# Output chunks gathered before the first and between the first and second of seven products, and transpositions taken singly, in the gated blocks of a two-layer decoder

## The chip, the cores and the metric

The kernel runs on one core of one Trainium2 chip. The metric is the device time of one execution in microseconds; the figure given is the median of several runs. TensorE runs at one of two clock levels, 2.4 or 1.2 GHz.

## What is computed

The reference is a decoder of two layers with 256 tokens and width 1024, in float32. Each layer has a gated block (SwiGLU), an attention (stick-breaking in the first layer, sparse attention with three branches in the second), and another gated block. The change touches the four gated blocks alone:

```python
def _swiglu(x, w_in, w_out):
    a, b = jnp.split(x @ w_in, 2, axis=-1)
    return (jax.nn.silu(a) * b) @ w_out

h = h + 0.5 * _swiglu(_rmsnorm(h, ffn1_norm[layer]), ffn1_w_in[layer], ffn1_w_out[layer])
```

The inner width is 2816. The program names the gated blocks f10 and f20 (before and after the attention of layer 0), f11 and f21 (of layer 1).

## The kernel before

**Weights.** A unit is 128 rows by 1024 columns of float32, 512 KB. The class `Weights` loads units in one fixed order over SP's queue into five raw buffers (`wraw`, line 104). `pump` (line 146) makes two tiles of a unit: the upper part `wh` (ScalarE, line 166) and the lower part `wl`, the rest after rounding (VectorE, line 168). There are six buffers for each, so at most six units are converted ahead of TensorE, and a conversion waits until TensorE has used the unit six places before. The activations are split the same way, and a product is three matmuls for each piece of the sum: upper by upper, upper by lower, lower by upper (`mm3`, lines 222 to 224).

**Blocks.** The inner width has 11 blocks of 256. A plain block j takes four units and gives, for each half of the tokens, 256 gate and 256 value columns. `gate` (line 481) makes g = silu(.) * (.) of it: ScalarE's part at lines 487 and 490 (`sil`), VectorE's at lines 488 and 491. `gtrans` (line 494) transposes the block's g with four small matmuls into a bank `gTp` and evacuates it into an upper part (`gTh`, ScalarE, line 503) and a lower part (`gTl`, VectorE, line 504). These are the stationary operand of the second matrix.

**Pairs.** Two blocks j and j+1 are computed together by seven products in place of eight (`pair`, line 552). The activations are cut into four quarters (two halves of the tokens by two halves of the width), the weights into b11, b21 (block j) and b12, b22 (block j+1), two units each. A product is 12 matmuls of 128x512 on two units. p1 uses b11; p5 and p6 use kept sums of b11, b12, b22; p3 uses b22; p7 uses b12 + b22; p2 uses b21; p4 the last kept sum. The sums are made in two ways: a tile `keep` is loaded, converted, and then a DMA that GpSimd issues adds the next weight to it (line 133), and later VectorE adds to it (line 173). A conversion of `keep` therefore waits for such an addition. ScalarE's queue is in order, so everything behind that conversion waits too.

p1 and p2 go to a bank c11, p6 and p7 to cu (which first takes a copy of c11), p5 and p3 to c12, p4 to c21. Copies stand between: after p5 ScalarE copies c12 (line 582) before p3 adds to that bank; after p6 it copies cu before p7 adds to it; after p7 it copies cu to c21 (line 608) for p4. Four gates follow: of block j+1 after p6 and after p7, of block j after p2 and after p4.

**Output chunks.** A chunk (line 702) is one unit of the second matrix: 12 matmuls into the four banks of `o`. Chunk k reads the transposed g of block k // 2. TensorE has eight banks: four of the pool `acc`, which hold a pair's results until the output begins and the output from then on, two of pool `z`, two of `aux`. While the output is open, c11 and cu live in `z`, c12 and then c21 in one bank of `aux`, and all transpositions share the other.

**The order.** The table `FAST` (line 27) sets for each gated block the sequence. A number is a plain block; (j, n, m) and (j, n) with positive n is a pair that has the plain blocks n and m among its products; (j, -n) is a pair with n output chunks among its products. The same table gives the order of units (`fast`, line 229) and of the computation (`fast_blocks`, line 621). There are seven pairs with output chunks: two each in f10, f20 and f21 with seven chunks, one in f11 with six. In f10 the first of them follows the pair of blocks 3 and 4, in f20 and f21 that of blocks 2 and 3, in f11 plain block 7. `late` holds blocks whose g is not yet transposed; `trans` (line 638) transposes all of them. After a pair without chunks it holds two. `beside` runs side work of the attention that follows f11. The order written here is the program's; a scheduler with its own cost model then sets each engine's queue and may exchange neighbours.

Of the kernel before, what the change touches and what calls it, by code (L numbers as in the profile page):

```python
# [190 lines left out]
def build(tc, ctx, a, out):  # L191
# [37 lines left out]
    def fast(l):  # L229

        b = lambda j, k: [a[l[:2] + "i" + l[2]][4 * j + 2 * k + i] for i in range(2)]
        v, r, pairs = [], range(2), 0
        outs = [a[l[:2] + "o" + l[2]][i] for i in range(2 * NB)]
        for j in FAST[l]:
            if not isinstance(j, tuple):
                v += b(j, 0) + b(j, 1)
                continue
            j, *n = j
            b11, b21, b12, b22 = b(j, 0), b(j, 1), b(j + 1, 0), b(j + 1, 1)
            key = lambda i: (j, pairs % 2, i)  # L240
            kept = lambda last=False: [Sum(key(i), last=last) for i in r]
            u22 = [Unit(b22[i], key=key(i)) for i in r]
            tail_ = [Unit(b12[i], plus=b22[i]) for i in r] + [Unit(b21[i], key=key(i)) for i in r] + kept(True)
            v += [Sum(key(i), load=b11[i], then=b12[i]) for i in r]
            if n[0] < 0:
                c = lambda n: [outs.pop(0) for _ in range(n)]
                v += c(2) + kept() + c(1) + u22 + kept() + c(1) + tail_[0:2] + c(1) + tail_[2:4] + c(1) + tail_[4:6] + c(-n[0] - 6)
            elif len(n) == 2:
                v += b(n[0], 0) + b(n[0], 1) + kept() + b(n[1], 0) + u22 + kept() + b(n[1], 1) + tail_
            else:  # L250
                v += b(n[0], 0) + kept() + u22 + b(n[0], 1) + kept() + tail_
            pairs += 1
        if l == "f11":
            return v + outs
        v += outs
        units.extend(v)
# [206 lines left out]
    def ffn(l, hT, rs, post, targets, side=(), pool=None, start=None, room=new_room):  # L463
# [3 lines left out]
        with ExitStack() as es:  # L467
# [153 lines left out]
            def fast_blocks():  # L621
# [13 lines left out]

                    return first, second

                def trans():
                    while late:
                        gtrans(late.pop(0))  # L640

                def beside():
                    if side:
                        side.pop(0)()

                for j in FAST[l][2 if start else j0:]:
# [9 lines left out]
                    p1, p5, p3, p6, p7, p2, p4 = pair(j, q, n < 0)  # L656
                    if m:
                        p1(), trans()
                        f, g = block(n, [zbank("n") for _ in range(2)])
                        f(), g(), p5(), gtrans(n)  # L660
                        n, = m
                        f, g = block(n, [zbank("n") for _ in range(2)])
                        f(), p3(), p6(), g(), p7(), p2(), gtrans(n), p4()
                        late.append(j + 1)
                    else:
                        p1(), beside(), chunk(), trans(), chunk(), beside(), p5(), chunk(), beside(), p3(), p6(), beside()
                        chunk(), beside(), p7(), chunk(), p2(), chunk(), gtrans(j + 1), p4()
                        for _ in range(-n - 6):
                            chunk()
                    late.append(j)  # L670
                taken["one"] = False
                trans_last.extend(late)

            trans_last, late = [], [0, 1] if start else [j0 - 1]
# [27 lines left out]
            def chunk():  # L702
                ws.append(W.take())
                for t in range(2):
                    for hf in range(2):
                        mm(len(ws) - 1, t, hf)
                W.done()
                W.pump()

            fast_blocks()  # L710
            n = 2 * NB - 4
# [869 lines left out]
```

## Time and profile before

| | |
|---|---|
| median of 3 runs | 1040.67 us (1040.11 to 1043.32) |
| profiled execution | 1042.57 us, its span 1040.5 us |
| TensorE, matmuls | 1005.7 us busy, 97% of the span, 5033 instructions |
| TensorE, weight loads | 839.7 us (beside matmuls) |
| VectorE | 785.9 us |
| ScalarE | 660.0 us |
| GpSimd | 123.9 us |
| mean granted clock | 0.989 of 2.4 GHz |
| HBM read | 197.99 MB, 191 GB/s over the span |

A matmul of 128x512 takes about 0.39 us from its start to its modelled end, but the next one starts 0.227 us after it, since matmuls are pipelined. Starts, not durations, give the length of a stretch. The profile names engines PE (TensorE), PEld (its weight loads), DVE (VectorE), ACT (ScalarE), POOL (GpSimd) and SP (the queue that issues most DMAs), and leaves buffer numbers out of tile names. Idle time of TensorE stands in brackets behind a row, with what ended it.

### The profile page before, as it was taken

What the parts mean: (1) busy time and instruction counts of PE and PEld (TensorE: products, weight loads), DVE (VectorE), ACT (ScalarE), POOL (GpSimd) and SP (SyncE); (2) the same over time, 40 slices, a digit from 0 to 9 for tenths busy, and PEclk for the clock granted to TensorE, in tenths of its full rate; (3) what the DMA queues carried; (4) which work ended last, traced back from release to release, by engine and by line L of the source; (5) the groups of instructions that cost most, each with busy time, mean ns of one, the idle gap of its engine ahead of it and who ended that gap; (6) DMA issues with size and microseconds to landing.
All of it is one profiled execution on the core that took longest, in us unless ns stands there. A gap on an engine that the chain in (4) does not pass through costs nothing.

```text
span 1040.5 us, 14104 instructions
## 1 busy us (share of the span) xinstructions
PE 1005.7 (97%) x5033; PEld 839.7 (81%) x5033; DVE 785.9 (76%) x1077; ACT 660.0 (63%) x1043; POOL 123.9 (12%) x180
## 2 busy tenths in 40 slices
PE   9997999999999997999999999999989999979998
PEld 6785888898978876888888888788878888858887
DVE  7877778778869778885777678864798768768873
ACT  6755666677857656664555676653689746657651
POOL 0101000000001000100117111100056500010000
PEclk9998999999999999999999999999989999989999
DMA  8978778454336787787565667865441156887861
GB/s 324 316 214 226 208 214 263 135 192 140 123 122 208 211 247 205 187 256 224 184 200 158 203 203 226 239 213 158 146 145 38 41 178 187 228 221 203 236 225 40
DMA packets 57093, 199.95 MB, mean 192 GB/s; under 512 B 6464, under 2 KB 7488, under 8 KB 57024
## 3 DMA queue, kind: packets, MB, share of 16 engines
q1 hardware_dynamic: 50976, 177.93, 51.1%
q0 software_dynamic: 5760, 20.97, 12.0%
q8 instruction: 39, 0.64, 0.3%
q14 instruction: 30, 0.25, 0.1%
q10 hardware_dynamic: 288, 0.16, 0.1%
HBM read 197.99 MB, written 1.05 MB: 191 GB/s over the span
## 4 chain that ended last, share of the span: by engine, by line
PE 68%; DMA 9%; issue 7%; DVE 7%; ACT 5%; POOL 3%; SPq 0%; POOLq 0%; ACTq 0%; DVEq 0%
PE o L222 8%; PE o L224 8%; PE o L223 8%; DVE wl L168 3%; PE c L222 3%; PE c L223 3%; PE c L224 3%; DMA wraw<-in_f1i 3%; DMA keep<-in_f1i 3%; ACT wh L166 2%; DMA wraw<-in_f2i 2%; PE a L224 2%; PE a L222 2%; PE a L223 2%; DMA keep<-in_f2i 2%
## 5 line engine op out<-in xcount | busy, mean ns | idle before, releaser
L168 DVE TENSOR_TENSOR wl<-wraw,wh 128x1024 fp32r<-128x1024 f32 (+2 forms) x310 | 374.0, 1218 | 111.2 <-ACT wh L166 108.0
L166 ACT ACTIVATE wh<-wraw 128x1024 fp32r<-128x1024 f32 (+2 forms) x312 | 322.2, 1045 | 150.7 <-PE o L224 54.2
L166 ACT ACTIVATE wh<-keep 128x1024 fp32r<-128x1024 f32 x80 | 84.3, 1057 | 62.3 <-DMA keep<-in_f2i 24.6
L168 DVE TENSOR_TENSOR wl<-keep,wh 128x1024 fp32r<-128x1024 f32 x80 | 97.4, 1222 | 27.1 <-ACT wh L166 25.8
L222 PE MATMUL o<-wh,gTh0f 128*128 128x512 f32 x192 | 76.6, 399 | 5.4 <-DVE g L491 5.4
L222 PE MATMUL a<-wh,hT_f 128*128 128x512 f32 x192 | 76.1, 396 | 0.0
L223 PE MATMUL o<-wl,gTh0f 128*128 128x512 f32 x192 | 75.3, 392 | 0.0
L224 PE MATMUL o<-wh,gTl0f 128*128 128x512 f32 x192 | 75.1, 391 | 0.0
L224 PE MATMUL a<-wh,hT_f 128*128 128x512 f32 x192 | 75.0, 390 | 0.0
L223 PE MATMUL a<-wl,hT_f 128*128 128x512 f32 x192 | 75.0, 390 | 0.0
L222 PE MATMUL o<-wh,gTh1f 128*128 128x512 f32 (+1 forms) x160 | 62.7, 392 | 0.0
L224 PE MATMUL o<-wh,gTl1f 128*128 128x512 f32 (+1 forms) x160 | 62.0, 388 | 0.0
L223 PE MATMUL o<-wl,gTh1f 128*128 128x512 f32 (+1 forms) x160 | 61.9, 387 | 0.0
L173 DVE TENSOR_TENSOR keep<-keep,wraw 128x1024 f32<-128x1024 f32 x40 | 48.7, 1221 | 15.2 <-DMA wraw<-in_f2i 11.2
L342 POOL TENSOR_TENSOR rstd<-rss,mhalf 128x1 f32<-128x1 f32 x12 | 8.4, 704 | 364.8 <-DVE rss L340 364.8
L222 PEld LDWEIGHTS o<-wh,gTh0f 128*128 128x128 f32 x192 | 36.3, 189 | 13.8 <-DVE g L491 6.7
L222 PE MATMUL n<-wh,hT_f 128*128 128x512 f32 x112 | 44.3, 395 | 0.0
L224 PE MATMUL n<-wh,hT_f 128*128 128x512 f32 x112 | 43.7, 390 | 0.0
L223 PE MATMUL n<-wl,hT_f 128*128 128x512 f32 x112 | 43.6, 390 | 0.0
L498 PE MATMUL gTp<-cst,g 128*128 128x128 f32 x176 | 28.0, 284 | 15.6 <-DVE gTl0f L504 15.0
L224 PEld LDWEIGHTS o<-wh,gTl0f 128*128 128x128 f32 x192 | 36.3, 189 | 7.7
L224 PEld LDWEIGHTS a<-wh,hT_f 128*128 128x128 f32 x192 | 36.1, 188 | 7.6
(352 smaller groups left out, 2467.8 us busy)
## 6 DMA issues: line engine op xcount, KB each, us to landing
wraw<-in_f1i SPq DMA_DIRECT2D x76, 512.0 KB, 4.5
wraw<-in_f2i SPq DMA_DIRECT2D x76, 512.0 KB, 4.4
wraw<-in_f1o SPq DMA_DIRECT2D x44, 512.0 KB, 4.4
wraw<-in_f2o SPq DMA_DIRECT2D x44, 512.0 KB, 4.5
wraw<-in_sbqk SPq DMA_DIRECT2D x16, 512.0 KB, 3.4
keep<-in_f2i SPq DMA_DIRECT2D x12, 512.0 KB, 5.0
keep<-in_f2i POOLq DMA_DIRECT2D x12, 512.0 KB, 7.4
wraw<-in_f2i POOLq DMA_DIRECT2D x12, 512.0 KB, 5.9
```

Of the source, the lines that this page charges most:

```text
L166: nc.scalar.activation(hi[:, 0:n], raw[:, 0:n], AF.Copy)
L168: e.tensor_tensor(lo[:, 0:n], raw[:, 0:n], hi[:, 0:n].bitcast(F32), op=OP.subtract)
L173: nc.vector.tensor_tensor(t, t, raw, op=OP.add)
L222: nc.tensor.matmul(o, xh, wh, start=start, stop=False, skip_group_check=True)
L223: nc.tensor.matmul(o, xh, wl, start=False, stop=False, skip_group_check=True)
L224: nc.tensor.matmul(o, xl, wh, start=False, stop=stop, skip_group_check=True)
L342: nc.gpsimd.tensor_tensor(r[:, 0:1], s, mhalf[:, 0:1], op=OP.pow)
L498: nc.tensor.transpose(p[:, c * 256 + t * P:c * 256 + (t + 1) * P], gs[j, t][:, c * P:(c + 1) * P], ident)
```

## The change

The chunks of a pair move. Before, one stood behind each of p1, p5, p6, p7, p2, with a second one before p5 and the last ones at the end. Now n - 5 chunks (two, in f11 one) come ahead of p1, four between p1 and p5, one between p6 and p7, and none elsewhere. The order of the units follows. `trans` takes a number: between p1 and p5 one transposition is made after the first of the four chunks and one after the third, where before two were made together after the first chunk. Block j of a pair without chunks is put at the front of `late`. f11's side work has six places in a pair in place of five.

```diff
@@ -241,10 +241,10 @@
             kept = lambda last=False: [Sum(key(i), last=last) for i in r]
             u22 = [Unit(b22[i], key=key(i)) for i in r]
             tail_ = [Unit(b12[i], plus=b22[i]) for i in r] + [Unit(b21[i], key=key(i)) for i in r] + kept(True)
-            v += [Sum(key(i), load=b11[i], then=b12[i]) for i in r]
+            c = lambda n: [outs.pop(0) for _ in range(n)]
+            v += c(max(-n[0] - 5, 0)) + [Sum(key(i), load=b11[i], then=b12[i]) for i in r]
             if n[0] < 0:
-                c = lambda n: [outs.pop(0) for _ in range(n)]
-                v += c(2) + kept() + c(1) + u22 + kept() + c(1) + tail_[0:2] + c(1) + tail_[2:4] + c(1) + tail_[4:6] + c(-n[0] - 6)
+                v += c(4) + kept() + u22 + kept() + c(1) + tail_
             elif len(n) == 2:
                 v += b(n[0], 0) + b(n[0], 1) + kept() + b(n[1], 0) + u22 + kept() + b(n[1], 1) + tail_
             else:
@@ -635,8 +635,8 @@
 
                     return first, second
 
-                def trans():
-                    while late:
+                def trans(n=2):
+                    for _ in range(min(n, len(late))):
                         gtrans(late.pop(0))
 
                 def beside():
@@ -662,12 +662,15 @@
                         f, g = block(n, [zbank("n") for _ in range(2)])
                         f(), p3(), p6(), g(), p7(), p2(), gtrans(n), p4()
                         late.append(j + 1)
+                        late.insert(0, j)
                     else:
-                        p1(), beside(), chunk(), trans(), chunk(), beside(), p5(), chunk(), beside(), p3(), p6(), beside()
-                        chunk(), beside(), p7(), chunk(), p2(), chunk(), gtrans(j + 1), p4()
-                        for _ in range(-n - 6):
+                        for _ in range(-n - 5):
                             chunk()
-                    late.append(j)
+                        p1(), beside()
+                        for _ in range(2):
+                            chunk(), trans(1), chunk(), beside()
+                        p5(), p3(), beside(), p6(), beside(), chunk(), beside(), p7(), p2(), gtrans(j + 1), p4()
+                        late.append(j)
                 taken["one"] = False
                 trans_last.extend(late)
```

**TensorE, start of f10's first pair with chunks.** c21 is p4 of the pair before, c11 is p1, o00 the first quarter of a chunk (the number behind wh is the unit), gTp a transposition, c12 is p5. Before:

```order
L222 MATMUL c21_779<-wh33_786,hT_0_120 128x512
...
L222 MATMUL c11_878<-wh34_798,hT_0_120 128x512
...
L222 MATMUL o00_874<-wh36_829,gTh0f10_442 128x512
...
L498 MATMUL gTp_920<-cst_78,g_731 128x128
...
L222 MATMUL o00_874<-wh37_852,gTh0f10_442 128x512
...
L498 MATMUL gTp_927<-cst_78,g_834 128x128
...
L222 MATMUL c12_953<-wh38_864,sums_385 128x512
```

Now:

```order
L222 MATMUL c21_779<-wh33_786,hT_0_120 128x512
...
L222 MATMUL o00_878<-wh34_798,gTh0f10_442 128x512
...
L222 MATMUL o00_878<-wh35_817,gTh0f10_442 128x512
...
L222 MATMUL c11_914<-wh36_829,hT_0_120 128x512
...
L222 MATMUL o00_878<-wh38_868,gTh0f10_442 128x512
...
L498 MATMUL gTp_957<-cst_78,g_837 128x128
...
L222 MATMUL o00_878<-wh39_894,gTh0f10_442 128x512
...
L222 MATMUL o00_878<-wh40_910,gTh0f10_442 128x512
...
L498 MATMUL gTp_1000<-cst_78,g_731 128x128
...
L222 MATMUL o00_878<-wh41_922,gTh0f10_442 128x512
...
L222 MATMUL c12_1026<-wh42_934,sums_385 128x512
```

Two chunks stand ahead of p1, and two chunks stand between the transpositions in place of one.

**ScalarE, the same place.** `wh<-keep` is a conversion of a kept unit, sil_870 and sil_874 the gate after p4, cu the copy after p1. Before:

```order
L166 ACTIVATE wh37_852<-wraw37_803 128x1024
L503 ACTIVATE gTh1f10_842<-gTp_837 128x512
L166 ACTIVATE wh38_864<-keep_761 128x1024
L490 ACTIVATE sil_870<-c21_779,rstd_348 128x256
L166 ACTIVATE wh39_886<-keep_773 128x1024
L166 ACTIVATE wh40_898<-wraw40_856 128x1024
L575 ACTIVATE cu_879<-c11_878 128x512
L166 ACTIVATE wh41_915<-wraw41_868 128x1024
L166 ACTIVATE wh42_946<-wraw42_890 128x1024
L503 ACTIVATE gTh0f10_442<-gTp_920 128x512
```

Now:

```order
L166 ACTIVATE wh37_855<-keep_802 128x1024
L503 ACTIVATE gTh1f10_845<-gTp_840 128x512
L166 ACTIVATE wh38_868<-wraw38_821 128x1024
L490 ACTIVATE sil_874<-c21_779,rstd_348 128x256
L166 ACTIVATE wh39_894<-wraw39_834 128x1024
L166 ACTIVATE wh40_910<-wraw40_860 128x1024
L166 ACTIVATE wh41_922<-wraw41_872 128x1024
L166 ACTIVATE wh42_934<-keep_790 128x1024
L575 ACTIVATE cu_915<-c11_914 128x512
L166 ACTIVATE wh43_953<-keep_802 128x1024
L166 ACTIVATE wh44_976<-wraw44_926 128x1024
L503 ACTIVATE gTh0f10_442<-gTp_957 128x512
```

The first conversion that waits for an accumulating DMA (wh38 before, wh42 now) has moved from ahead of the gate to four conversions behind it.

**TensorE and ScalarE, p5 to p4 of that pair, now.** On TensorE c12 is p5 and p3, cu is p6 and p7, c11 is p2, c21 is p4; g_1105 and g_1155 are the gates of block j+1 after p6 and after p7:

```order
L222 MATMUL c12_1026<-wh42_934,sums_385 128x512
...
L222 MATMUL cu_915<-wh46_1019,sums_385 128x512
...
L222 MATMUL c12_1026<-wh44_976,sums_385 128x512
...
L222 MATMUL cu_915<-wh47_1033,sums_385 128x512
...
L498 MATMUL gTp_1187<-cst_78,g_1105 128x128
L222 MATMUL c21_1126<-wh53_1120,hT_0_120 128x512
...
L222 MATMUL c21_1126<-wh54_1133,hT_0_120 128x512
L498 MATMUL gTp_1187<-cst_78,g_1155 128x128
```

On ScalarE, from the copy after p7 to the gate's part:

```order
L608 ACTIVATE c21_1126<-cu_915 128x512
L166 ACTIVATE wh56_1164<-wraw56_1124 128x1024
L166 ACTIVATE wh57_1176<-keep_1137 128x1024
L487 ACTIVATE sil_1154<-x_1152,rstd_348 128x256
L490 ACTIVATE sil_1183<-c11_914,rstd_336 128x256
```

The chunk between p5 and p3 is gone, and the scheduler has put the first four matmuls of p6 there; behind p7 two chunks are gone, and one of the four transpositions and seven matmuls of p4 stand ahead of the other three.

## Rows read from the trace of the kernel before

**Rows 1.** The page, parts 1 and 2: busy time of the engines (share of the span, instructions), and TensorE's granted clock in 40 slices of the span, in tenths.

```profile
PE 1005.7 (97%) x5033; PEld 839.7 (81%) x5033; DVE 785.9 (76%) x1077; ACT 660.0 (63%) x1043; POOL 123.9 (12%) x180
PEclk9998999999999999999999999999989999989999
```

**Rows 2.** The list of waits, TensorE's alone: the waiting line and what it waited for, us in total, times, longest.

```profile
PE gTp L498 <- DVE gTl0f L504: 15.0, 3, 5.8
PE o L222 <- DVE g L491: 5.4, 3, 2.6
```

**Rows 3.** The instructions in order of time, TensorE: start and duration in us, line, tiles, and in brackets the idle time before it and what ended it. f10, f10, f20, f20, f21, f21.

```profile
92.09 0.80 PE L222 MATMUL o<-wh,gTh0f 128*128 128x512 f32 x1 [2.63 <-DVE g L491]
101.42 0.66 PE L498 MATMUL gTp<-cst,g 128*128 128x128 f32 x4 [3.76 <-DVE gTl0f L504]
389.57 0.50 PE L222 MATMUL o<-wh,gTh0f 128*128 128x512 f32 x1 [1.66 <-DVE g L491]
399.24 1.11 PE L498 MATMUL gTp<-cst,g 128*128 128x128 f32 x4 [5.48 <-DVE gTl0f L504]
921.72 0.50 PE L222 MATMUL o<-wh,gTh0f 128*128 128x512 f32 x1 [1.12 <-DVE g L491]
931.62 1.12 PE L498 MATMUL gTp<-cst,g 128*128 128x128 f32 x4 [5.75 <-DVE gTl0f L504]
```

**Rows 4.** The table by stretches: from and to in us, length, busy us of each engine (instructions), granted clock (1.00 is 2.4 GHz), DMA share, GB/s.

```profile
91.70:95.10 3.40, 3.01 (x9) 2.52 (x10) 1.71 (x3) 1.33 (x2) 0.00 (x0) 0.50 0.74 264
102.00:105.40 3.40, 3.40 (x10) 2.63 (x10) 2.24 (x3) 1.26 (x2) 0.89 (x1) 0.51 0.85 282
398.90:402.30 3.40, 3.06 (x10) 2.58 (x11) 3.15 (x4) 0.60 (x1) 0.87 (x1) 0.50 0.95 337
928.00:934.80 6.80, 3.18 (x10) 2.70 (x11) 6.43 (x7) 2.52 (x4) 0.86 (x1) 0.50 0.90 254
```

**Rows 5.** In order of time, ScalarE at the start of the first pair with chunks in f10.

```profile
90.16 1.06 ACT L166 ACTIVATE wh<-keep 128x1024 fp32r<-128x1024 f32 x1 [4.67 <-DMA keep<-in_f1i]
93.77 1.06 ACT L166 ACTIVATE wh<-keep 128x1024 fp32r<-128x1024 f32 x1 [2.19 <-DMA keep<-in_f1i]
98.09 0.57 ACT L503 ACTIVATE gTh0f<-gTp 128x512 fp32r<-128x512 f32 x1
```

**Rows 6.** In order of time, TensorE: the first transposition of such a pair, in f10 and in f21.

```profile
93.54 1.06 PE L498 MATMUL gTp<-cst,g 128*128 128x128 f32 x4
922.52 0.60 PE L498 MATMUL gTp<-cst,g 128*128 128x128 f32 x4
```

**Rows 7.** In order of time, f10, f20 and f21: the matmul that follows p4's last (TensorE), and the lower part of the transposition before p4 (VectorE).

```profile
84.54 0.39 PE L222 MATMUL c<-wh,hT 128*128 128x512 f32 x1
87.14 0.68 DVE L504 TENSOR_TENSOR gTl1f<-gTp,gTh1f 128x512 fp32r<-128x512 f32 x1
383.00 0.39 PE L222 MATMUL c<-wh,hT_f 128*128 128x512 f32 x1
384.47 0.69 DVE L504 TENSOR_TENSOR gTl0f<-gTp,gTh0f 128x512 fp32r<-128x512 f32 x1
915.68 0.39 PE L222 MATMUL c<-wh,hT_f 128*128 128x512 f32 x1
916.40 0.69 DVE L504 TENSOR_TENSOR gTl0f<-gTp,gTh0f 128x512 fp32r<-128x512 f32 x1
```

**Rows 8.** In order of time, f21: the lower part of the second chunk's unit (VectorE), the issue of the second accumulating DMA (GpSimd), the conversion that waited for its landing (ScalarE).

```profile
915.27 1.23 DVE L168 TENSOR_TENSOR wl<-wraw,wh 128x1024 fp32r<-128x1024 f32 x1
913.96 0.88 POOL L133 DMA_DIRECT2D keep<-in_f2i  x1 [0.88 <-DVE wl L168]
923.97 1.06 ACT L166 ACTIVATE wh<-keep 128x1024 fp32r<-128x1024 f32 x1 [2.76 <-DMA keep<-in_f2i]
```

**Rows 9.** In order of time: start of p7 and of the chunk after it (f10), the issue after p5's last matmul (f20), the copy after p5 (f20).

```profile
117.13 0.39 PE L222 MATMUL cu<-wh,sums 128*128 128x512 f32 x1
119.85 0.39 PE L222 MATMUL o<-wh,gTh0f 128*128 128x512 f32 x1
403.91 0.39 PE L222 MATMUL o<-wh,gTh0f 128*128 128x512 f32 x1
404.11 0.60 ACT L582 ACTIVATE cp<-c 128x512 f32<-128x512 f32 x1 [0.26 <-PE c L224]
```

**Rows 10.** In order of time, p7 in f10's first pair with chunks: a conversion that waited for the first half of p7, the gate's two parts after p7; then f20's pair without chunks: the matmul after p7's last, and the gate's second part.

```profile
118.75 1.06 ACT L166 ACTIVATE wh<-keep 128x1024 fp32r<-128x1024 f32 x1 [0.31 <-PE cu L224]
121.70 0.51 ACT L487 ACTIVATE sil<-x,rstd 128x256 f32<-128x256 f32 x1
122.78 0.42 DVE L488 SCALAR_TENSOR_TENSOR g<-x,sil 128x256 f32<-128x256 f32 x1
377.06 0.39 PE L222 MATMUL c<-wh,hT_f 128*128 128x512 f32 x1
382.67 0.43 DVE L488 SCALAR_TENSOR_TENSOR g<-x,sil 128x256 f32<-128x256 f32 x1
```

**Rows 11.** The page, part 5: groups by line, engine and tiles, count, busy us and mean ns of one, idle before and its releaser.

```profile
L166 ACT ACTIVATE wh<-keep 128x1024 fp32r<-128x1024 f32 x80 | 84.3, 1057 | 62.3 <-DMA keep<-in_f2i 24.6
L168 DVE TENSOR_TENSOR wl<-keep,wh 128x1024 fp32r<-128x1024 f32 x80 | 97.4, 1222 | 27.1 <-ACT wh L166 25.8
L173 DVE TENSOR_TENSOR keep<-keep,wraw 128x1024 f32<-128x1024 f32 x40 | 48.7, 1221 | 15.2 <-DMA wraw<-in_f2i 11.2
```

## The prediction

> **What bounds the kernel now.** I read the page first. Matmuls keep TensorE busy for 1005.7 of the 1040.5 us of the span, VectorE for 785.9 [rows 1]. TensorE is the bound, the diff neither adds nor removes a matmul, and so the change can only move the 34.8 us in which TensorE stands, and its clock: the clock line shows a dip in four slices inside the span.
>
> The second view is the list of TensorE's waits. Two entries hold 20.4 of the 34.8 us, each three times [rows 2]: transpositions that wait for the lower part of an earlier transposition (15.0), and output chunks that wait for a gate (5.4). TensorE's rows in order of time place all six [rows 3]: they lie in f10, f20 and f21, each time at the start of the first pair with output chunks: the first chunk waits 2.63, 1.66 and 1.12 us, and one chunk later the second of two transpositions waits 3.76, 5.48 and 5.75 us. The later pairs and f11 show none of these.
>
> The third view is the table by stretches, for the clock. After four of the six waits the granted clock is 0.50, which is 1.2 GHz in place of 2.4, with 3.01, 3.40, 3.06 and 3.18 us of matmuls in those stretches [rows 4]. Half of these 12.65 us, 6.3 us, is lost. After the waits of 1.66 and 1.12 us it did not fall by itself. The prize is thus 20.4 + 6.3 = 26.7 us.
>
> Why these waits are so long is read on ScalarE and VectorE. The gate that frees the last output bank stands behind the conversion of a kept unit, and that one stands 4.67 us until its accumulating DMA has landed; the next stands another 2.19 us, and the first transposition, on TensorE at 93.54, is evacuated only at 98.09 [rows 5, 6]. With one bank for transpositions the second one waits for all of this.
>
> **The change part by part.** All products and chunks take 119.85 - 117.13 = 2.72 us at full clock [rows 9]. I count from p4's end in the pair before.
>
> The first chunk now follows p4 directly, where p1 stood between. Three quarters of it (2.04 us) go to banks that are free; the last quarter needs p4's own gate. The gate no longer stands behind an accumulating DMA: ahead of it is now the conversion of a plain chunk unit. So it is VectorE's queue that decides, where the gate follows the lower part of a transposition. f10: TensorE is there at 84.54 + 2.04 = 86.6, the gate ends at 87.14 + 0.68 + 0.42 = 88.2, a wait of 1.7. f20: 385.0 against 384.47 + 0.69 + 0.42 = 385.6, 0.5. f21: 917.7 against 917.5, none [rows 7]. Together 2.2 us; bounds 0 (the gate in time) and 5.4 (as now).
>
> The transpositions come one at a time, with two chunks between them: 2 x 2.72 + 0.36 = 5.8 us of matmuls. The new risk is in f20 and f21: their fifth chunk reads block 2, whose transposition has moved to one chunk ahead of it. Its evacuation queues on VectorE behind the kept unit a1 and the additions to it. In f21 the slot at 915.27 on VectorE, now a1's, ends at 916.5; then the accumulating DMA is issued, which took 913.96 to 923.97, 10.0 us; landing is at 926.5 [rows 8]. A conversion (1.06), a lower part (1.22), an addition (1.22) [rows 11] and the evacuation's 0.69 give 930.7. The chunk is due at 915.68 + 5 x 2.72 + 0.36 = 929.6: a wait of 1.0. f20 is taken alike: 2.0 us. Bounds: 0, if the DMA takes the 7 us of the shorter ones, and the wait of today, if nothing gets quicker. I stay near zero, because the four units ahead on ScalarE are now plain ones and the accumulation is asked for four chunks, not two, before p5 wants it. In f10 the first transposition is read only after p6.
>
> [...] The change adds no bank. [...]
>
> p5, p3 and p6 lose the chunk that stood between p5 and p3. p3 adds to the bank that ScalarE copies after p5: the copy starts 0.20 us after the last issue of p5 and takes 0.60 [rows 9], so p3 could come 0.86 us late, seven times. But the order shows four matmuls of p6 (4 x 0.227 = 0.91 us) ahead of p3. They cover it: 0. Without this cover it is 6.0 us.
>
> p7, p2 and p4 lose both chunks. The transposition of block j+1 needs the gate behind p7. It had 8.2 us of cover; now p2 (2.72), one transposition (0.09) and seven matmuls of p4 (1.59): 4.40. The chain from p7's end: ScalarE copies c21, converts one unit, then a second that waits for the first half of p2 (a conversion starts 0.26 us after such a half, row at 118.75 [rows 9, 10]): 1.36 + 0.26 + 1.06 = 2.7. VectorE then ends the lower part before it at 3.0, this one at 4.2, the gate at 4.6. The wait is 0.2 us, in seven pairs 1.4. Two measured chains bound it: with one conversion between, 122.78 + 0.42 - 119.85 = 3.35 (no wait); in f20's block pair, where VectorE was behind, 382.67 + 0.43 - 377.06 = 6.04, a wait of 1.6 [rows 10]. I take the replay, since VectorE is not behind here: four chunks before p5 need 1.22 us of it per 2.72 us.
>
> SP issues the same loads; a1's and a0's accumulations move two units later on POOL's queue, costed above. The last chunk behind each second pair is gone to its front; block 10 or the remaining chunks follow p4 without a dependence that is late.
>
> Sum: 26.7 - 2.2 - 2.0 - 0 - 1.4 = 21.1 us. The profiled execution took 1042.57 us, 2.07 more than its span and 1.9 above the median of the runs, 1040.67. I take the saving off the median: **1019.5 us**.
>
> **The rivals.**
> First, the room is still too short. The time from the first transposition to the second was 101.42 - 93.54 = 7.9 us in f10 and 931.62 - 922.52 = 9.1 in f21 [rows 3, 6]. If it stays, f10 waits 7.9 - 5.8 = 2.1, and f20's and f21's fifth chunk, with 3.1 us of cover, 6.0 each; the clock falls after these two as it did, 3.2 us. That is 17.3 in place of 2.0: 1035. For it: one bank, and an accumulation that takes 10 us. Against: in those 9 us ScalarE stood for two DMAs that now have landed, or nearly.
>
> Second, VectorE is behind in p7 and p2, since p5 to p4 now carry six products on 12 units with one chunk. Then the chain is 6.04, 1.64 us of wait seven times in place of 0.2: 1029.5.
>
> Third, slower: the weights do not keep up between p5 and p4. There TensorE runs 7 x 2.72 + 0.36 = 19.4 us, while VectorE has 13 lower parts and 4 additions of 1.22, 4 gates of 0.42 and three pieces of 0.69 (two sums taken like the transposition) [rows 7, 10, 11]: 24.5 us. The difference of 5.1 us must stand ready in the six buffers when p5 begins, about four units. With none, seven pairs lose 36 us: 1055. It turns the result from 3.0 us per pair on, so with fewer than two units ready. Against it: in the six products and chunks before, VectorE needs far less than TensorE.
>
> **How the numbers follow.** My forecast gets 0.62, VectorE behind 0.16, the short room 0.15, weights too late 0.04; 0.03 is left for waits that only change their place, near 1040. A measurement of this kernel tells 0.3%, 3.1 us, from no change. Faster: 0.62 + 0.16 + 0.15 = 0.93; same 0.03; slower 0.04. With no new wait at all it is 1014.0; the 34.8 us of rows 1 hold more small waits, so the low end is 1011. The forecast and the second rival hold only 0.78, so the range goes on to the first rival's 1035.
>
> **What would show it.** Right: the list of TensorE's waits has lost the entry of 15.0 us, or keeps under 3; chunk waits on gates of about 2 us, in f10 above all; no stretch at clock 0.50 in f10 and f20; ScalarE's waits for kept units shorter. Each pair shows p3 without a wait and the second transposition after p7 up to 0.5 us late. Wrong: waits of output chunks or transpositions for gTl0f of over 2 us (first rival), waits for g at L498 of over 1 us in seven places (second), waits for wl at L222 or L223 in the pairs (third).

## The result, and the profile after

The changed kernel takes **1026.13 us** (median; 1024.75 to 1027.33) against 1041.05 us of the kernel before measured beside it; the ratio is 0.9853, with a 95% interval of 0.9831 to 0.9875. That is 6.6 us above the forecast of 1019.5, and two thirds of the way from there to the second rival's 1029.5 (VectorE behind in p7 and p2). The two profiled executions differ by 16.9 us in span, 1040.5 and 1023.6.

The page of the changed kernel, for [rows 1]: TensorE's busy time, its clock in 40 slices, and the additions to kept units, for [rows 11].

```profile
PE 1002.1 (98%) x5033; PEld 834.5 (82%) x5033; DVE 785.1 (77%) x1077; ACT 659.3 (64%) x1043; POOL 123.3 (12%) x180
PEclk9999999999999999999999999999999999999999
L173 DVE TENSOR_TENSOR keep<-keep,wraw 128x1024 f32<-128x1024 f32 x40 | 48.9, 1224 | 32.7 <-DMA wraw<-in_f2i 21.3
```

No slice of the clock's line is under nine tenths any more. Note the third row: the additions are as many and as long as before, but VectorE now stands 32.7 us ahead of them, where it stood 15.2.

The list of TensorE's waits, for [rows 2] (us in total, times, longest):

```profile
PE gTp L498 <- DVE g L488: 8.1, 5, 2.3
PE o L223 <- DVE wl L168: 0.5, 1, 0.5
PE c L222 <- ACT cp L582: 0.5, 1, 0.5
PE o L222 <- DVE g L491: 0.2, 1, 0.2
```

The entry of 15.0 us (transposition for an earlier lower part) is not there any more; of the 5.4 us of chunks waiting for gates 0.2 is left. In their place stands a new one of 8.1 us: transpositions for the gate behind p7. In order of time (start, duration, idle time before it): f10; f20 twice; f21 twice.

```profile
125.08 0.90 PE L498 MATMUL gTp<-cst,g 128*128 128x128 f32 x3 [2.28 <-DVE g L488]
418.48 0.55 PE L498 MATMUL gTp<-cst,g 128*128 128x128 f32 x3 [1.91 <-DVE g L488]
460.58 0.55 PE L498 MATMUL gTp<-cst,g 128*128 128x128 f32 x3 [2.30 <-DVE g L488]
944.23 0.55 PE L498 MATMUL gTp<-cst,g 128*128 128x128 f32 x3 [0.58 <-DVE g L488]
984.66 0.55 PE L498 MATMUL gTp<-cst,g 128*128 128x128 f32 x3 [1.05 <-DVE g L488]
```

The two transpositions at the start of f10's first pair with chunks, for [rows 3, 6], TensorE and then ScalarE (the second kept unit, the first evacuation):

```profile
94.59 0.60 PE L498 MATMUL gTp<-cst,g 128*128 128x128 f32 x4
100.50 0.60 PE L498 MATMUL gTp<-cst,g 128*128 128x128 f32 x4
...
94.98 1.06 ACT L166 ACTIVATE wh<-keep 128x1024 fp32r<-128x1024 f32 x1 [2.33 <-DMA keep<-in_f1i]
...
96.89 0.58 ACT L503 ACTIVATE gTh0f<-gTp 128x512 fp32r<-128x512 f32 x1
```

ScalarE stands 2.33 us for an accumulation in place of 4.67 and 2.19 [rows 5], the first bank is read out 4.6 us after its transposition (VectorE's part ends at 99.16) and not 7.9 us, and 5.9 us of matmuls cover it: no wait.

The clock, by stretches (length, TensorE busy, granted clock, DMA share, GB/s), for [rows 4]: behind the waits of 2.28 us in f10, 1.91 and 2.30 us in f20.

```profile
125.08:128.50 3.42, 3.42 (x10) 0.54 0.82 212
418.48:421.90 3.42, 3.42 (x17) 1.00 0.88 210
460.58:464.00 3.42, 3.42 (x17) 1.00 0.95 327
```

In the pairs the granted clock fell to 0.50 once (0.54 over that stretch), where it fell in four places before [rows 4]; 0.46 x 3.42 = 1.6 us are lost. Both kernels have one more such fall, in the attention of layer 1 (774 to 782 us before, 762 to 770 now, 0.57 over either stretch), which the change does not touch. Taken in windows of 0.25 us, the granted clock of both traces is 1.00 or 0.50, and in between only where one turns into the other.

The sum, from the two traces: 20.4 - 0.2 us of waits gone, 6.3 of clock back, less 8.1, 0.5 and 0.5 of new waits and 1.6 of clock: 15.8 us. The other 1.1 us of the 16.9 were not followed one by one; small entries of the list that have nothing to do with the pairs fell by more than that (one alone, of 1.5 us for kcT in the attention, is gone).

**Where the new wait comes from.** VectorE in f10's first pair with chunks, in order of time. L173 is an addition to a kept unit, L168 a lower part, L587 a sum out of PSUM, L488 the gate that the transposition reads. p7 ended on TensorE at 118.21.

```profile
102.99 0.68 DVE L504 TENSOR_TENSOR gTl0f<-gTp,gTh0f 128x512 fp32r<-128x512 f32 x1
108.04 1.23 DVE L173 TENSOR_TENSOR keep<-keep,wraw 128x1024 f32<-128x1024 f32 x1 [4.37 <-DMA wraw<-in_f1i]
109.18 1.22 DVE L168 TENSOR_TENSOR wl<-keep,wh 128x1024 fp32r<-128x1024 f32 x1
110.43 1.23 DVE L173 TENSOR_TENSOR keep<-keep,wraw 128x1024 f32<-128x1024 f32 x1
111.58 5.76 DVE L168 TENSOR_TENSOR wl<-wraw,wh 128x1024 fp32r<-128x1024 f32 x5
117.25 0.68 DVE L587 TENSOR_TENSOR x<-c,cp 128x512 f32<-128x512 f32 x1
...
121.75 0.68 DVE L587 TENSOR_TENSOR x<-cu,cp 128x512 f32<-128x512 f32 x1
122.34 1.22 DVE L168 TENSOR_TENSOR wl<-wraw,wh 128x1024 fp32r<-128x1024 f32 x1
123.48 1.22 DVE L168 TENSOR_TENSOR wl<-keep,wh 128x1024 fp32r<-128x1024 f32 x1
124.61 0.42 DVE L488 SCALAR_TENSOR_TENSOR g<-x,sil 128x256 f32<-128x256 f32 x1
```

From 103.67 to 108.04 VectorE does nothing: the next instruction in its queue is an addition whose unit is still being loaded. After that it never stands again up to the gate, which comes 6.8 us behind p7's end. The order of its instructions tells what stood behind the addition (unit 51's load is what it waits for; units 47 to 50 are needed sooner):

```
108 L168 TENSOR_TENSOR wl46_1020<-keep_790,wh46_1019 128x1024
109 L504 TENSOR_TENSOR gTl0f10_443<-gTp_1000,gTh0f10_442 128x512
110 L173 TENSOR_TENSOR keep_790<-keep_790,wraw51_1050 128x1024
111 L168 TENSOR_TENSOR wl47_1034<-keep_802,wh47_1033 128x1024
112 L173 TENSOR_TENSOR keep_802<-keep_802,wraw52_1064 128x1024
113 L168 TENSOR_TENSOR wl48_1047<-wraw48_998,wh48_1046 128x1024
```

VectorE keeps to this order: in the 4.37 us none of the lower parts behind the addition started, though ScalarE had ended the upper part of the next one at 105.02. All seven pairs, from such rows:

| pair | VectorE stands at the additions | p7's end to the gate's end | wait of the transposition |
|---|---|---|---|
| f10, first | 4.37 | 6.82 | 2.28 |
| f10, second | 1.15 | 4.47 | none |
| f20, first | 3.19 | 6.45 | 1.91 |
| f20, second | 4.11 | 6.83 | 2.30 |
| f11 | 1.48 | 4.48 | none |
| f21, first | 0.61 + 1.29 | 5.15 | 0.58 |
| f21, second | 2.47 | 5.62 | 1.05 |

The room, from p7's end to where the transposition is due, is about 4.5 us everywhere. Where the addition stood less than 1.5 us the chain is 4.5 us, the 4.6 of the prediction's replay; it grows with the standing. That VectorE comes late because it stood at the addition is **theory 1**. **Theory 2** is the prediction's second and third rival put together: from p5 to p4 VectorE has more work than TensorE (24.5 against 19.4 us), and would be behind in any order.

### The profile page after: what moved, and what is told of

The parts are those of the page before. It is cut to its first block, busy times and chain, and to the rows that moved or that the text cites. A ratio compares the mean times of both kernels' runs of the same rounds, so it can differ in the third digit from the quotient of the medians.

```text
span 1023.6 us, 14113 instructions
## 1 busy us (share of the span) xinstructions
PE 1002.1 (98%) x5033; PEld 834.5 (82%) x5033; DVE 785.1 (77%) x1077; ACT 659.3 (64%) x1043; POOL 123.3 (12%) x180
## 3 DMA queue, kind: packets, MB, share of 16 engines
HBM read 197.99 MB, written 1.05 MB: 194 GB/s over the span
## 4 chain that ended last, share of the span: by engine, by line
PE 71%; DVE 11%; DMA 7%; issue 5%; POOL 3%; ACT 3%; SPq 0%; DVEq 0%; ACTq 0%; POOLq 0%
PE o L222 7%; PE o L223 7%; PE o L224 7%; DVE wl L168 6%; PE a L222 3%; PE a L224 3%; PE a L223 3%; PE n L223 3%; PE n L224 3%; PE n L222 3%; DMA wraw<-in_f1i 3%; PE c L224 2%; PE c L223 2%; PE c L222 2%; ACT wh L166 2%
## 5 line engine op out<-in xcount | busy, mean ns | idle before, releaser
L168 DVE TENSOR_TENSOR wl<-wraw,wh 128x1024 fp32r<-128x1024 f32 (+2 forms) x310 | 372.3, 1217 | 103.0 <-ACT wh L166 100.9
L168 DVE TENSOR_TENSOR wl<-keep,wh 128x1024 fp32r<-128x1024 f32 x80 | 97.6, 1220 | 14.1 <-ACT wh L166 12.5
L222 PE MATMUL o<-wh,gTh0f 128*128 128x512 f32 x192 | 76.3, 398 | 0.2 <-DVE g L491 0.2
L222 PE MATMUL a<-wh,hT_f 128*128 128x512 f32 x192 | 76.0, 396 | 0.0
L224 PE MATMUL o<-wh,gTl0f 128*128 128x512 f32 x192 | 75.0, 391 | 0.1
L224 PE MATMUL a<-wh,hT_f 128*128 128x512 f32 x192 | 74.9, 390 | 0.0
L173 DVE TENSOR_TENSOR keep<-keep,wraw 128x1024 f32<-128x1024 f32 x40 | 48.9, 1224 | 32.7 <-DMA wraw<-in_f2i 21.3
L222 PE MATMUL o<-wh,gTh1f 128*128 128x512 f32 (+1 forms) x160 | 62.7, 392 | 0.0
L224 PE MATMUL o<-wh,gTl1f 128*128 128x512 f32 (+1 forms) x160 | 62.0, 387 | 0.0
L222 PE MATMUL n<-wh,hT_f 128*128 128x512 f32 x112 | 44.3, 396 | 0.0
L224 PE MATMUL n<-wh,hT_f 128*128 128x512 f32 x112 | 43.7, 390 | 0.0
L223 PEld LDWEIGHTS o<-wl,gTh0f 128*128 128x128 f32 x192 | 36.2, 189 | 8.1 <-DVE wl L168 0.9
L224 PEld LDWEIGHTS o<-wh,gTl0f 128*128 128x128 f32 x192 | 36.0, 188 | 8.2 <-DVE gTl0f L504 0.6
L222 PEld LDWEIGHTS o<-wh,gTh0f 128*128 128x128 f32 x192 | 36.2, 189 | 7.9 <-DVE g L491 0.6
L224 PEld LDWEIGHTS a<-wh,hT_f 128*128 128x128 f32 x192 | 36.1, 188 | 7.7
```

Of the source, the lines that this page charges most:

```text
L168: e.tensor_tensor(lo[:, 0:n], raw[:, 0:n], hi[:, 0:n].bitcast(F32), op=OP.subtract)
L173: nc.vector.tensor_tensor(t, t, raw, op=OP.add)
L222: nc.tensor.matmul(o, xh, wh, start=start, stop=False, skip_group_check=True)
L223: nc.tensor.matmul(o, xh, wl, start=False, stop=False, skip_group_check=True)
L224: nc.tensor.matmul(o, xl, wh, start=False, stop=stop, skip_group_check=True)
```

## The experiments

Twelve kernels, each timed beside the kernel before; ratios are to it.

**1. Which part of the change brings the gain?** First the transpositions apart, with the chunks where they were:

```
-p1(), beside(), chunk(), trans(), chunk(), beside(), p5(), chunk(), beside(), p3(), ...
+p1(), beside(), chunk(), trans(1), chunk(), beside(), p5(), trans(1), chunk(), beside(), p3(), ...
```

> The kernel before with one part of the change: the second transposition moves behind p5, so that a chunk and a product lie between the two; the chunks stay where they were (the first one behind p1). If the two transpositions standing together were all that cost, the entry of 15.0 us goes to under 2 and the clock stays up: about 1021 us. If the first evacuation is as late as before (the second transposition could start 7.9 to 9.1 us after the first), 5.8 us of matmuls cover only part: some 2 to 3 us of wait in each of f10, f20 and f21, and the chunk's wait for the gate, 5.4 us, is not touched: about 1031 us.

Measured: 1034.69 us, 0.9922 (0.9896 to 0.9948). Its list of TensorE's waits:

```profile
PE gTp L498 <- DVE gTl0f L504: 7.3, 3, 2.4
...
PE o L222 <- DVE g L491: 2.0, 3, 0.9
```

The second transposition still waits 2.44 us in each of f10, f20 and f21: the evacuation is as late as before and the distance covers only part of it, as expected there. Not as expected, the chunks' waits for a gate fell too, from 5.4 to 2.0 us. Then the chunks alone, with both transpositions behind the third chunk:

```
-for _ in range(2):
-    chunk(), trans(1), chunk(), beside()
+chunk(), trans(), chunk(), beside()
+chunk(), chunk(), beside()
```

> The changed kernel with its chunks where they are, but with both transpositions asked for after the third chunk; by the order some 2.3 us of matmuls lie between them. In the changed kernel the first evacuation ends 4.6 us (f10) and 3.9 us (f20) after its transposition starts. If that is what the second one would wait for, it waits 1.9 us in f10 and about 1.2 us in f20 and f21: 4 us in all, with one fall of the clock at the most, 1030 us. If moving the chunks alone did the work, no wait of over 0.5 us appears: 1026 us. If the waits of before come back (3.8 to 5.8 us each), 1041 us.

Measured: 1032.99 us, 0.9886 (0.9855 to 0.9917).

```profile
PE gTp L498 <- DVE g L488: 9.5, 6, 2.3
PE gTp L498 <- DVE gTl0f L504: 3.3, 3, 1.5
```

The transpositions wait 3.3 us in three places (0.78, 1.06, 1.49), near the 4 expected: moving the chunks has made the evacuation early, but not early enough for two transpositions close together. So each part alone gives some 8 and 12 us by the ratios, and only both together leave the second transposition without a wait; the wait for the gate behind p7 (9.5 here) comes with the chunks, not with the transpositions.

**2. The standing addition.** The additions are held behind the lower part of their own unit, in all ten pairs; their work stays the same:

```
-nc.vector.tensor_tensor(t, t, raw, op=OP.add)
+self.tc.keep_in_program_order(nc.vector.tensor_tensor(t, t, raw, op=OP.add))
```

> The changed kernel with VectorE's additions to the kept units held behind the lower part of their own unit; the same work, but no addition stands in VectorE's queue for a load that the next conversions do not need. Theory 1, VectorE is behind after p7 because it stood 0.6 to 4.4 us at an addition whose unit was still being loaded: the five waits of the transposition for the gate, 8.1 us, fall below 2 us in all and the clock stays up in f10: about 1017.5 us. Theory 2, VectorE is behind because from p5 to p4 it has more work (24.5 us) than TensorE (19.4): the waits stay above 6 us: about 1025 us.

Measured: 1028.50 us, 0.985 (0.982 to 0.9879): no better than the change, a miss in time. The trace shows why the time says little. TensorE, f10's transposition of block j+1 (no wait now), then f20's pair without chunks and the chunk after it:

```profile
124.68 0.55 PE L498 MATMUL gTp<-cst,g 128*128 128x128 f32 x3
...
370.38 0.50 PE L222 MATMUL cu<-wh,sums 128*128 128x512 f32 x1 [1.96 <-ACT cp L582]
377.48 0.55 PE L498 MATMUL gTp<-cst,g 128*128 128x128 f32 x3 [1.26 <-DVE g L491]
385.35 0.50 PE L222 MATMUL o<-wh,gTh0f 128*128 128x512 f32 x1 [1.73 <-DVE g L491]
```

All five waits for the gate behind p7 are gone, as theory 1 says and theory 2 does not, but holding the additions has put new waits into the pairs with blocks. So the same edit in the seven pairs with chunks alone:

```
-u22 = [Unit(b22[i], key=key(i)) for i in r]
+u22 = [Unit(b22[i], key=key(i), pin=n[0] < 0) for i in r]
```

(and so for the units of b21; only a unit with pin holds its addition.)

> The changed kernel with the additions held behind their own unit's lower part in the seven pairs with output chunks alone; the pairs with blocks keep their order. Theory 1 (VectorE stands at an addition whose unit is not there yet): as in the run with all additions held, no transposition after p7 waits over 0.3 us, and the waits that holding them brought into the pairs with blocks (1.75, 1.73, 1.96, 1.26 us) are not there: 1026.1 - 8.1 - 1.7 = 1016.3 us. Theory 2 (VectorE has too much work from p5 to p4, whatever the order): no better than with all held, 1026 us or more.

Measured: **1018.74 us**, 0.9779 (0.9761 to 0.9797). No transposition behind p7 waits over 0.3 us (0.25 and 0.28 in two pairs); the longest entry of the pairs is this one, the first chunks' waits for gates:

```profile
PE o L224 <- DVE g L493: 2.0, 3, 1.1
```

(With this edit all lines behind the addition stand two further down: L224 is the L222 of the other kernels, L493 their L491, L500 their L498.) Theory 1 is right within 2.5 us, and those are mostly this entry. VectorE has exactly the work of the changed kernel, and in f10's first pair it does both additions ahead of the gate as there; yet from p7's end to the gate's end it now takes 4.16 to 4.38 us in the six pairs of f10, f20 and f21, where it took 4.47 to 6.83. So theory 2 falls.

**3. A longer room for the gate.** One chunk goes from ahead of p5 to between p7 and p2:

```
-for _ in range(2):
-    chunk(), trans(1), chunk(), beside()
-p5(), p3(), beside(), p6(), beside(), chunk(), beside(), p7(), p2(), gtrans(j + 1), p4()
+chunk(), trans(1), chunk(), beside(), trans(1), chunk(), beside()
+p5(), p3(), beside(), p6(), beside(), chunk(), beside(), p7(), chunk(), p2(), gtrans(j + 1), p4()
```

(The order of units follows.)

> The changed kernel with three chunks in place of four between p1 and p5 and the fourth put between p7 and p2, which gives the gate 2.72 us more. Both theories of the gate behind p7 have the waits there (2.28, 1.91, 2.30, 0.58, 1.05) at zero: about 1017 us, unless the shorter distance between the two transpositions (a chunk less) costs: then up to 2 us in f10, at L498 for gTl0f, 1019 us. If the gate waits for something that moves along with p2 (a conversion that p2's buffers free), the waits stay: 1026 us.

Measured: 1047.91 us, 1.0042 (1.0023 to 1.0061): slower than before, and 22 to 31 us above every time that I had expected. Its waits, and VectorE in f10's second pair with what TensorE did then:

```profile
PE cu L223 <- DVE wl L168: 8.4, 3, 3.6
PE gTp L498 <- DVE gTl0f L504: 6.0, 3, 2.2
PE gTp L498 <- DVE g L488: 4.9, 4, 1.9
PE c L222 <- ACT cp L582: 3.9, 1, 3.9
...
153.41 1.23 DVE L173 TENSOR_TENSOR keep<-keep,wraw 128x1024 f32<-128x1024 f32 x1 [5.93 <-DMA wraw<-in_f1i]
154.55 1.22 DVE L168 TENSOR_TENSOR wl<-keep,wh 128x1024 fp32r<-128x1024 f32 x1
...
155.82 0.80 PE L223 MATMUL cu<-wl,sums 128*128 128x512 f32 x1 [2.48 <-DVE wl L168]
```

The addition now stands 5.93 us, and behind it is the lower part that p6 itself needs: TensorE waits for weights. If that is the cause, holding the additions must take most of it away in this kernel too.

> The slow kernel (a chunk between p7 and p2, 1048 us) with the additions of the pairs with chunks held behind their own unit's lower part. Theory 1: that kernel is slow because its additions stand longer (4.2 to 6.5 us), so the waits of p6 and of the chunks for lower parts (9.1 us in four), of p7's transposition (4.9) and of the copy in f11 (3.9) go, with their falls of the clock; what stays is the short distance of the two transpositions, 6.0 us and one or two falls of the clock: 1026 us, and at the most 1030. If a chunk less ahead of p5 leaves TensorE without weights, whatever the additions do: over 1040 us.

Measured: 1030.46 us, 0.9889 (0.9875 to 0.9904), some 16 us less by the same edit. What stays is the short distance of the two transpositions:

```profile
PE gTp L500 <- DVE gTl0f L506: 8.5, 3, 4.0
```

**4. Was the addition also the cause of the old waits?** The same edit in the kernel before:

> The kernel before with the additions of the pairs with chunks held in the same way. If the six waits of 20.4 us come from the places of the chunks and transpositions alone, they stay: 1040 us, within 4. If the standing addition was also what made these waits, they fall: under 1030 us.

Measured: 1040.96 us, 0.9993 (0.9981 to 1.0004); the entry for gTl0f is 16.4 us, that of the chunks 4.4. It was not: the change took away what it aimed at, and met something else.

**5. A later reader of the gate.** The transposition of block j+1 goes from between p2 and p4 to the next pair's chunks:

```
-p7(), p2(), gtrans(j + 1), p4()
-late.append(j)
+p7(), p2(), p4()
+late.extend([j + 1, j])
```

(A leading chunk is followed by a transposition while more than two blocks wait for theirs.)

> The changed kernel with the transposition of block j+1 taken out from between p2 and p4 and put among the first chunks of the next pair (or the remaining chunks); additions as in the changed kernel, so VectorE still stands and is still behind. If the wait is only that the gate comes late for that one reader, it has 8 us more and waits no more: 8.1 us and one fall of the clock go, 1017 us. If VectorE's lag holds up others too (the first chunk's last bank waits for p4's gate, a chunk waits for lower parts): part of it comes back there, 1020 to 1026 us.

Measured: 1023.09 us, 0.9819 (0.9798 to 0.984), the second of the two cases. No transposition waits for the gate behind p7 any more. In its place the two transpositions behind f10's second pair wait 1.2 us for another gate (L491), weights are late by 1.5 us in two places and a copy by 1.2. With the additions held as well:

> Both remedies: additions held behind their own unit's lower part in the pairs with chunks, and the transposition of block j+1 among the next pair's first chunks. With either alone hardly a wait is left (2.0 us of the chunks for gates with the first, 3.3 us of gates and lower parts with the second), so both together bring no more than these: 1017 to 1019 us.

Measured: 1022.84 us, 0.9804 (0.9778 to 0.983), not better than either, and by the ratio 2.6 us worse than holding them alone, though the intervals just overlap. Now transpositions that stand close together wait for one another again (4.2 us for gTl1f in six, three of them in second pairs, and 2.9 of chunks for what they carry). The two remedies don't add.

**6. Why is the load late?** In f10 the loads of the two units that the additions want are issued here, at 100.37 and 101.45, when lower parts that end at 100.29 and 101.43 have given their buffers back, and the addition that needs the first of them starts at 108.04, 7.7 us later, with the two accumulations of 98.02 and 99.33 on the DMA engines at the same time:

```profile
100.37 1.41 SPq L104 DMA_DIRECT2D wraw<-in_f1i  x2
```

In the kernel before, the load for the addition in the same place was issued later and yet was there when VectorE came to it (no idle time ahead of the addition):

```profile
102.56 0.33 SPq L104 DMA_DIRECT2D wraw<-in_f1i  x1
...
106.97 1.22 DVE L173 TENSOR_TENSOR keep<-keep,wraw 128x1024 f32<-128x1024 f32 x1
```

So: two buffers more for loaded units, one pair less for converted ones.

```
-W = Weights(tc, wp, units, raws=5, bufs=6)
+W = Weights(tc, wp, units, raws=7, bufs=5)
```

> The changed kernel with seven buffers for loaded units in place of five, and five pairs of buffers for converted units in place of six (the same memory); the additions stand in VectorE's queue as in the changed kernel. If the addition stands because its unit's load could only start when a lower part gave a buffer back (in f10 at 100.37, landed at 108.0), the load starts two units earlier, the addition stands under 1.5 us, and the waits of 8.1 us go: 1018 us, plus what one converted unit less costs (up to 4 us, at lower parts). If the load is late because the DMA queues are full, the addition stands as long as now: 1026 us or more.

Measured: **1017.74 us**, 0.9753 (0.9728 to 0.9779), with the held additions (0.9779) the fastest; the two intervals overlap. The additions' row of its page, and TensorE's only wait in a pair with chunks over 0.5 us:

```profile
L173 DVE TENSOR_TENSOR keep<-keep,wraw 128x1024 f32<-128x1024 f32 x40 | 48.9, 1222 | 0.9
...
912.87 0.50 PE L224 MATMUL o<-wh,gTl0f 128*128 128x512 f32 x1 [0.62 <-DVE gTl0f L504]
```

The order stays much as it was, the additions still stand ahead of other lower parts, but they find their units there: 0.9 us in place of 32.7, and from p7's end to the gate's end it takes 4.5 us in each of the six pairs of f10, f20 and f21. In the pairs with chunks the converted unit less costs nothing that shows. Outside of them two new waits may belong to it: 1.7 us for converted weights in the first plain blocks (b at L519), and 4.1 us in place of 1.7 ahead of one transposition in the attention of layer 1 (pt). Their cause is not shown. The same exchange in the kernel before:

> The kernel before with seven buffers for loaded units and five pairs for converted ones, in place of five and six; chunks and transpositions as before. If the six waits of 20.4 us come from where the chunks and transpositions stand (one bank for transpositions, the gate behind kept units whose accumulating DMA has not landed), they stay over 15 us, with their falls of the clock: about 1038 us. If earlier loads alone would heal them too, they fall under 6 us: about 1020 us, and the change of order was not needed.

Measured: 1063.49 us, 1.0191 (1.0167 to 1.0215). The chunks wait for no gate now, but the three waits for gTl0f grow from 15.0 to 23.5 us, and in f11 a transposition waits 5.4 us for side work (hidT). GpSimd's queue and ScalarE in f10 show what goes ahead of that evacuation:

```profile
82.43 0.89 POOL L133 DMA_DIRECT2D wraw<-in_f1i  x1 [20.51 <-DVE wl L168]
82.98 2.14 POOL L133 DMA_DIRECT2D keep<-in_f1i  x2
...
93.79 1.06 ACT L166 ACTIVATE wh<-keep 128x1024 fp32r<-128x1024 f32 x1 [8.06 <-DMA keep<-in_f1i]
```

With an earlier load, an accumulation into a loaded unit gets ahead of the two into kept units, and ScalarE stands 8.06 us for these, where it stood 4.67 [rows 5]. The same exchange gives 8 to 10 us in one order and costs 20 in the other.

**7. The additions on GpSimd** (in the seven pairs), which takes them off VectorE's queue and work:

```
-nc.vector.tensor_tensor(t, t, raw, op=OP.add)
+(nc.gpsimd if x.pin else nc.vector).tensor_tensor(t, t, raw, op=OP.add)
```

> The changed kernel with the additions of the seven pairs with chunks done by GpSimd: nothing stands in VectorE's queue, and VectorE has 4.9 us less work in each of these pairs. Theory 1 (only the standing counts): the same as with the additions held in place, 1018.7 us, with no transposition after p7 waiting over 0.3 us. Theory 2 (the amount of VectorE's work counts as well): less than that, 1015 us. GpSimd's own addition is slower (2.4 us for such a tile in this trace) and the accumulating DMAs are issued behind it: if that decides, waits for kept units appear on ScalarE and the time is over 1022 us.

Measured: 1049.97 us, 1.007 (1.0044 to 1.0096). VectorE and GpSimd in f10's first pair:

```profile
100.89 6.58 DVE L168 TENSOR_TENSOR wl<-wraw,wh 128x1024 fp32r<-128x1024 f32 x1
...
100.36 2.73 POOL L173 TENSOR_TENSOR keep<-keep,wraw 128x1024 f32<-128x1024 f32 x1
...
103.32 3.06 POOL L173 TENSOR_TENSOR keep<-keep,wraw 128x1024 f32<-128x1024 f32 x1
```

One lower part takes 6.58 us in place of 1.22, about as long as GpSimd's two additions. The run says nothing between the theories: VectorE did not get its queue free.

## Why the prediction came out as it did

- **The six waits (20.4 us) and the clock (6.3):** right. 0.2 us and one new fall of the clock are left. A misreading beside it changes no sum: the clock line of [rows 1] dips in three slices, not four, and the middle one is the attention's; f20's fall shows in [rows 4] alone.
- **The first chunk's last quarter, 2.2 us:** too dear; 0.2, in f20 alone. VectorE reached the gate earlier in f10: the lower part ahead of it began at 84.34, not 87.14 [rows 7], while TensorE was earlier by 0.8 us only.
- **The fifth chunk of f20 and f21, 2.0 us:** too dear; none. In these two first pairs no conversion waited for an accumulation (1.9 us at the most elsewhere in f20 and f21), which fits the four plain units now ahead of the kept one.
- **p3's copy, 0:** right in six pairs; 0.5 us in f11. (0.20 and 0.60 of [rows 9] add to 0.80; no row shows the rest of the 0.86. The forecast of 0 does not use it.)
- **The transposition behind p7, 7 x 0.2 = 1.4 us: this is the step that failed.** It cost 8.1 us in five pairs, with 1.6 us of clock and 0.5 us of one late weight. The room was right (4.40 forecast, 4.5 measured) and so was the replay of the chain (4.6; 4.47 and 4.48 where the addition stood least, 1.15 and 1.48 us). Wrong was its condition, "VectorE is not behind here", for which only VectorE's work was counted. It was behind by standing: an addition in its queue asks for a load that SyncE issued only when a buffer came free (in f10 at 100.37, 0.08 us behind the end of a lower part). The row for it was there, in [rows 11]: 15.2 us of idle time ahead of the additions, 11.2 of them ended by loads of f2's weights alone; I took from this row the duration only. Nor did I read the order around the additions: in the kernel before, the one of unit 49 stood ahead of the lower parts of 45 to 48, with its load in time.
- **The first rival (room too short):** did not come in the changed kernel; how near it is shows in the 7.3 us of waits with the chunks left behind p1, and in the 8.5 us with one chunk less between the transpositions. A second bank for transpositions was not needed, and the time of about 1035 did not come: with one bank 5.9 us of other matmuls were enough in f10, where the first was read out after 4.6.
- **The second (VectorE behind in p7 and p2):** came in five of seven pairs, at 0.58 to 2.30 us against 1.64. Its reason, six products with one chunk among them, was wrong; the additions held in the seven pairs and the seven buffers keep the work and have no such wait.
- **The third (weights too late):** not in the changed kernel, but the chunk behind p7 made it come, over the same addition: p6 waited 8.4 us for lower parts.

What goes with such standing could be read in the kernel before. Of the 15.2 us 8.8 lie in the pairs without chunks and 6.1 in the second pairs of f10, f20 and f21, where the addition stood 2.55, 2.42 and 1.15 us. There p7's end to the gate's end took 5.70, 5.75 and 4.44 us, against 3.34 or 3.35 in the three first pairs, where none stood; f10's second pair:

```profile
149.05 1.22 DVE L173 TENSOR_TENSOR keep<-keep,wraw 128x1024 f32<-128x1024 f32 x1 [2.55 <-DMA wraw<-in_f1i]
158.92 0.39 PE L222 MATMUL o<-wh,gTh0f 128*128 128x512 f32 x1
164.21 0.41 DVE L488 SCALAR_TENSOR_TENSOR g<-x,sil 128x256 f32<-128x256 f32 x1
```

The 6.04 us that the prediction took as its upper bound come from a pair in which an addition had stood 1.99 us.

The losses forecast were 2.2 + 2.0 + 1.4 = 5.6 us; measured 0.2 + 0.5 + 8.1 + 1.6 + 0.5 = 10.9. That makes 5.3 of the 6.6 us; the rest is within what the runs differ by. That the time came as near as it did is in part luck: the first two terms were too dear by 4.0 us together and hid so much of the 8.8 us (10.2 less 1.4) that the failed step cost more than forecast.

What stays open: why the load came late in the changed order. The additions stand ahead of the lower parts of four earlier units in f10's first pair in both kernels, but before the load was in time. An earlier start heals it, as the seven buffers show; what held the load up on its way was not tried.

## What to carry to other kernels

VectorE, busy for 77% of the span, was still late, because one instruction in its queue asked for a load that had not come (4.37 us in f10's first pair); so for every queue on the path read the idle time ahead of each group and what ended it, not the busy time alone. An instruction that nobody needs soon must not stand ahead of those that are needed; hold it back, or make its input early (1018.74 and 1017.74 us here, in place of 1026.13). Look again at buffer numbers after a change of order: the same exchange gave 8 to 10 us after this change and cost 20 before it.

## What the runs showed of the hardware that I had not expected

- With the additions on GpSimd (experiment 7) VectorE was slower while GpSimd added: in f10's first pair a 128x1024 lower part took 6.58 us in place of 1.22 beside two additions and another 3.04 beside one (108.69 to 111.09), while one with none beside it (at 107.40) took 1.21. GpSimd's 28 additions took 2.91 us each in the mean, VectorE's own 1.22. What held VectorE up is not shown.
- The length of a wait did not tell whether the clock falls: the granted clock was 0.50 behind 2.28 us in f10, and 1.00 behind 2.30 and 1.91 us in f20, with like matmuls on both sides.
- Loads took longer beside accumulations. In the changed kernel 36 loads of 512 KB of the gated blocks were issued by SyncE with two or more accumulations on the way; they took 7.4 us to land (median), against 4.4 us for the 181 issued with none (before: 7.2 for 19 and 4.4 for 181). What else was on the way was not kept apart.
